# Two fused blocks on one core: priorities at the norm boundaries, and new places for masks, norm rows, zero stores and decay scalars

## The chip, the cores and the metric

The kernel runs on one core of a Trainium2 chip. The metric is device time in microseconds of one execution. The kernel before has a median of 932.28 us over three runs, between 931.84 and 934.05.

## The reference

One sequence of 256 tokens, each of 1024 float32 values, goes through two blocks. The first has attention with a relative bias and a gated delta rule beside it, both from one projection, then an MLP with squared relu. The second has a short convolution and a retention mixer, then a gated MLP. In short:

```python
# first block
h    = rms_norm(x, pre_mix_norm)
proj = h @ w_in                       # att q,k,v; gdn q,k,v; z; a; b
o    = concat(attention(att_q, att_k, att_v, rel_bias), gated_deltanet(...))
x    = x + rms_norm(o @ w_out, post_mix_norm)
x    = x + rms_norm(square(relu(rms_norm(x, pre_mlp_norm) @ w_up)) @ w_down, post_mlp_norm)
# inside gated_deltanet, in chunks of 64 tokens, 8 heads of 64
q, k, v = split(silu(causal_conv(qkv)))
q, k    = l2_normalize(q) / 8, l2_normalize(k)
g       = -exp(A_log) * softplus(a + dt_bias);  beta = sigmoid(b)
m       = strict_lower((k * beta) @ k.T * decay(g))
u, w    = solve(I + m, [v * beta, k * beta * exp(cumsum(g))])
# then a scan over the chunks: state, v_new = u - w @ state, output
# second block
h = rmsnorm(x, g_mix);  proj = h @ w_in_2
y_a = (gb * conv3(gc * xc)) @ w_a_out
y_r = (groupnorm(retention(rotary(q), rotary(k), v, log_sigmoid(dec_f), log_sigmoid(dec_b))) * g_ret * silu(g_sw)) @ w_r_out
x = x + (sigmoid(gate_a) * y_a + sigmoid(gate_r) * y_r) @ w_o
h = rmsnorm(x, g_ffn);  x = x + (silu(h @ w_ff_gate) * (h @ w_ff_up)) @ w_ff_down
return rmsnorm(x, g_final)
```

## The kernel before

Every matrix product is made of three: a float32 operand is split into a rounded part and a remainder, hi and lo, and hi*hi, hi*lo and lo*hi are added in PSUM (mm3, L222 and L294). Weights come in chunks of 512 KB. load_w (L208) issues the transfer to the tile raw on SyncE's queue, ScalarE copies raw to wh (the rounded part), VectorE subtracts to get wl (the remainder). Three buffers hold raw, six each wh and wl, so the transfer of a chunk starts when ScalarE and VectorE are through with the third chunk before it.

A scheduler puts the instructions of the whole program in order on each engine by priority, which falls with the place in the source; an engine then works through its own list strictly in order. Two things bend this order. `with after("x")` orders an instruction behind the one last recorded as `last["x"]` without making it wait for data (L170). And side work, the products of attention and of later projections, is cut into steps that go("q") or go(number) places between the steps of the mixer (the FILL list). The gates GATE_H and GATE_L order the splits of the first five chunks, the fifth behind the decay scalars g of the delta rule.

The mixer of the first block, 0 to about 190 us, runs as follows. The activations are normalised and transposed to xT. Projections for k and q are convolved (acc), turned back to tokens, squared (sq), summed (ssq, ssk), and their reciprocal norms are a power on POOL (rstd, L400: ms on VectorE, then rnk or rnq on POOL). VectorE forms m from the k products; m goes through DRAM (md) and comes back as mb, in blocks of 16. POOL scales k (kbe, kd, L876) and multiplies m with two level masks per token tile (b, L895, four instructions). VectorE scales q (fq, fqd, qn, qd) and solves the 16 by 16 blocks by substitution in 30 small steps (tmpb and tb, L937). The solution goes through the DRAM scratches td and ud and comes back as T and U (L947), for the products that join the blocks. Of td and ud only the diagonal blocks are written there; the zeros are stored at L828 from a tile of zeros, 520 KB each. A store to and a load from the same scratch are ordered by semaphores.

At three boundaries a product is followed by a norm whose result the next product needs: w_out to w_up (L1071), w_down to w_in_2 (L1120) and w_o_2 to the gated MLP (L1282). For each of the two token tiles, post_norm_add (L454) squares the sums on ScalarE, takes a power on POOL and adds to x on VectorE; rms_T (L444) repeats this for x and transposes the result on TensorE; split_T makes hi and lo on ScalarE and VectorE (xT, L413 and L416). The norm weights are rows broadcast over 128 partitions, two transfers of 256 KB each (row_bcast, L178), on POOL's queue, ordered behind the last power ("pow").

The logarithm of the second block's decays (log1p_exp_neg_abs, L497) stands behind the w_up products in the source; its ScalarE steps need a table for Ln, which a table load brings in.

Of the kernel before, what the change touches and what calls it, by code (L numbers as in the profile page):

```python
# [13 lines left out]
AF = mybir.ActivationFunctionType  # L14
ALU = mybir.AluOpType
# [82 lines left out]
def body(ctx: ExitStack, tc: tile.TileContext, I: dict, cst: bass.AP, out: bass.AP, dbg=None):  # L98
# [47 lines left out]
    def tt(o, a, b, op, eng=None):  # L146
        (eng or nc.vector).tensor_tensor(o, a, b, op=op)  # L147
# [21 lines left out]
    @contextmanager  # L169
    def after(what):  # L170

        if what in last:
            with tc.issue_after(last[what].ins):
                yield
        else:
            yield

    def row_bcast(name, eng=None):  # L178
        a = I[name]
        h = [xpool.tile([P, 512], F32, tag="wb", name=nm("wb"), bufs=4) for _ in range(2)]  # L180
        with after("pow"):
            for i in range(2):
                (eng or nc.gpsimd).dma_start(h[i], bass.AP(tensor=a.tensor, offset=a.offset + i * 512,
                                                           ap=[[0, P], [1, 512]]))
        return h
# [21 lines left out]

    def load_w(w, k0, nk, c0, ncol):  # L208
        raw = wpool.tile([P, nk, ncol], F32, tag="raw", name=nm("raw"), bufs=RBUFS)
        nc.sync.dma_start(raw, w[k0 * P:(k0 + nk) * P, c0:c0 + ncol].rearrange("(k p) n -> p k n", p=P))  # L210
        H = wpool.tile([P, nk, ncol], F32R, tag="wh", name=nm("wh"), bufs=WBUFS)
        L = wpool.tile([P, nk, ncol], F32R, tag="wl", name=nm("wl"), bufs=WBUFS)
        n = len(started)
        started.append(1)
        with after(GATE_H[n] if n < len(GATE_H) else None):
            act(H, raw, AF.Copy)
        with after(GATE_L[n] if n < len(GATE_L) else "sub"):
            last["wl"] = nc.vector.tensor_tensor(L, raw, H.bitcast(F32), op=SUB)  # L218
        return H, L
# [180 lines left out]
    def rstd(o, ss, n, dim):  # L400
        ms = sm("ms", n)
        nc.vector.tensor_scalar(ms, ss, 1.0 / dim, EPS, op0=MUL, op1=ADD)
        tt(o, ms, neghalf[:, :n], ALU.pow, nc.gpsimd)

    def split_T(ps, X, k0, t, scale=None):

# [35 lines left out]
        return xs  # L442

    def rms_T(xt, wb, X, t):  # L444
        row_T(rms_row(xt, wb, t in FUSED), X, t)

    def row_T(row, X, t):
        for i, xs in enumerate(row):
# [3 lines left out]
            split_T(ps, X, 4 * i, t)  # L452

    def post_norm_add(ps, wb, xt):  # L454
        r = rms_of(ps)
        tmp = [T2("pw", tag="n") for _ in range(2)]
        for i in range(2):
            tt(tmp[i], ps[i], wb[i], MUL)
        for i in range(2):
            stt(xt[:, GS[i]], tmp[i], r, xt[:, GS[i]], MUL, ADD)  # L460

    xr = [rms_row(x[:, t, :], wb_pre, True, None) for t in range(2)]
    C0 = T2("cs")
# [28 lines left out]
        return h  # L492

    hs = head_scalars(("A_log", "dt_bias"))
    load_consts(0, NMIX)

    def log1p_exp_neg_abs(src, n):  # L497

        a, u, w, l, d, rw = (sm("lp" + c, n) for c in "auwldr")
        act(a, src, AF.Abs)  # L500
        act(u, a, AF.Exp, scale=-1.0)
        nc.vector.tensor_scalar(w, u, 1.0, None, op0=ADD)
        last["ln"] = nc.scalar.activation(l, w, AF.Ln)
        stt(d, w, -1.0, u, ADD, SUB)
        nc.vector.reciprocal(rw, w)
        tt(d, d, rw, MUL)
        tt(l, l, d, SUB)
        return l
# [315 lines left out]


    KBE, KD, KT_, MM, BL = [], [], [], [], []
    for d in (td, ud):
        nc.sync.dma_start(d[:, :].rearrange("p (r n) -> p r n", r=5),  # L828
                          zero[:, None, :208].to_broadcast([P, 5, 208]))
    pk = [tok_major(2, t) for t in range(2)]  # L830
    rk = [inv_norm(pk[t], "k") for t in range(2)]
    go(FILL[2])
# [40 lines left out]
    for t in range(2):  # L873
        kbe, kd = G2("kbe"), G2("kd")
        tt(h8(kbe), h8(kn[t]), hb(tile_h(FB, t)), MUL, nc.gpsimd)
        tt(h8(kd), h8(kn[t]), hb(tile_h(ER, t)), MUL, nc.gpsimd)  # L876
        KBE.append(kbe)
        KD.append(kd)

    go("q")  # L880
    go(FILL[4])
    VB, AT, QDT = [], [], []
    pq = [tok_major(0, t) for t in range(2)]
    rq = [inv_norm(pq[t], "q") for t in range(2)]
# [6 lines left out]
    for t in range(2):  # L891
        bl = []
        for s in (16, 32):
            b = G2("b")
            tt(h8(b), h8(MM[t]), cb(f"lev{s}"), MUL, nc.gpsimd)  # L895
            bl.append(b)
        BL.append(bl)

# [167 lines left out]
    wout.rows(mix, 0, range(WT0, 8), True)  # L1066
    wout.rows(mix, 1, range(wout.k, 8))
    ps = wout.ps
    wb1, wb2 = row_bcast("post_mix_norm"), row_bcast("pre_mlp_norm")
    X = Both("xT")  # L1070
    for t in range(2):  # L1071
        post_norm_add(ps[t], wb1, x[:, t, :])
# [18 lines left out]
    for i in range(4, 16):  # L1091
        hf = G2("hf")

        def up_evac(i=i, hf=hf):
            r = G2("relu")
            act(r, hf, AF.Relu)
            stt(hf, hf, 0.0, r, MAX, MUL)
            hv = hf.rearrange("p (j n) -> p j n", j=2)
            act(hid.h[i], hv, AF.Copy)
            tt(hid.l[i], hv, hid.h[i].bitcast(F32), SUB)  # L1100

        gemm_wide(I["w_up"][0], 256 * i, X, hf, up_evac)
    load_consts(NMIX, 3)

    dl = head_scalars(("dec_f_2", "dec_b_2"))
    lg = sm("lg", 8)
    lp = log1p_exp_neg_abs(dl, 8)
    stt(lg, dl, 0.0, lp, ALU.min, SUB)
# [173 lines left out]
    for t in range(2):  # L1282
        for i in range(2):
            gs = slice(i * 512, (i + 1) * 512)
            tt(x[:, t, gs], ps[t][i], x[:, t, gs], ADD)
        rms_T(x[:, t, :], wb1, X, t)
    dump("x3", x[:, 0, :])

# [92 lines left out]
```

## Time and profile before

| what | value |
|---|---|
| median of three runs | 932.28 us |
| profiled execution | 932.19 us |
| its span | 930.4 us |
| mean granted TensorE clock | 0.994 |
| TensorE busy | 902.0 us, 97% |
| VectorE busy | 600.1 us, 64% |
| ScalarE busy | 475.2 us, 51% |
| POOL busy | 81.2 us, 9% |

The span is the time between the first and the last instruction that the profile shows; the profiled execution is 1.79 us longer. Busy shares are means over a span with stages of different limits. What an engine waits for is in the list of waits and, for single places, in the timeline, where the time in square brackets is the idle time before an instruction and the name behind the arrow what ended it. PE is TensorE, DVE is VectorE, ACT is ScalarE, SP is SyncE; a granted clock of 1.00 is 2.4 GHz and of 0.50 is 1.2 GHz.

### The profile page before, as it was taken

Reading aid. Unit: us, or ns where it says so; the run is one execution under the profiler, and the core shown is the slowest. Engines: PE = TensorE matmul, PEld = TensorE weight load, DVE = VectorE, ACT = ScalarE, POOL = GpSimd, SP = SyncE. Lnnn points to the kernel's source line nnn. Section 1 sums busy time; section 2 is a strip of 40 time slices with the busy share of each in tenths; the row PEclk is TensorE's granted clock in tenths of the full one; section 3 lists DMA queues with packets and bytes.
Section 4 is the critical chain, followed back from the end, with each engine's and each line's share of the span. In section 5 each row is a group of like instructions: output and inputs, shape, how many; then the busy total and the mean of one; then the engine's idle time right before and its main releaser. Section 6 shows DMA issues by size and latency. Waiting matters only on the chain.

```text
span 930.4 us, 13880 instructions
## 1 busy us (share of the span) xinstructions
PE 902.0 (97%) x5397; PEld 770.2 (83%) x5397; DVE 600.1 (64%) x885; ACT 475.2 (51%) x722; POOL 81.2 (9%) x96
## 2 busy tenths in 40 slices
PE   5999999989999999999999999999999999999997
PEld 4788887778888888799988888888888788888886
DVE  3888555376887563868666687844557657666543
ACT  4774373356766453645445555444344546555432
POOL 4072001030000000203200000000000000000000
PEclk9999999999999999999999999999999999999999
DMA  9673663147676665577646457666474567666551
GB/s 274 183 184 67 161 211 91 46 144 209 193 203 203 222 196 182 155 220 214 182 119 176 132 165 201 181 203 190 165 229 141 159 203 205 189 191 184 183 179 46
DMA packets 177138, 162.41 MB, mean 175 GB/s; under 512 B 18940, under 2 KB 144168, under 8 KB 177072
## 3 DMA queue, kind: packets, MB, share of 16 engines
q1 hardware_dynamic: 175200, 156.49, 57.3%
q0 software_dynamic: 1728, 4.78, 1.6%
q8 instruction: 42, 0.69, 0.3%
q10 hardware_dynamic: 144, 0.26, 0.1%
q14 instruction: 24, 0.20, 0.1%
HBM read 158.59 MB, written 2.92 MB: 174 GB/s over the span
## 4 chain that ended last, share of the span: by engine, by line
PE 85%; DMA 4%; POOL 3%; ACT 3%; DVE 3%; issue 2%; SPq 0%; POOLq 0%; ACTq 0%
PE mm L222 57%; PE at L222 18%; PE sd L222 6%; PE mm L294 2%; DMA raw<-in_w_in_dram 1%; POOL b L147 1%; ACT junk L424 1%; DVE wl L218 1%; PE sd L795 1%; POOL r L428 1%; DMA rows<-in_w_conv_dram 1%; DMA raw<-in_w_up_dram 1%; ACT wh L144 1%; DMA wb<-in_pre_mlp_norm_dram 1%; DMA x<-in_x_dram 0%
## 5 line engine op out<-in xcount | busy, mean ns | idle before, releaser
L218 DVE TENSOR_TENSOR wl<-raw,wh 128x1024 fp32r<-128x1024 f32 (+1 forms) x287 | 352.3, 1232 | 220.7 <-ACT wh L144 218.8
L144 ACT ACTIVATE wh<-raw 128x1024 fp32r<-128x1024 f32 (+1 forms) x287 | 301.8, 1056 | 293.5 <-PE at L222 69.5
L222 PE MATMUL mm<-xT,wh 128*128 128x256 f32 (+1 forms) x976 | 251.5, 334 | 1.4 <-ACT wh L144 1.4
L222 PEld LDWEIGHTS mm<-xT,wh 128*128 128x128 f32 x976 | 167.2, 193 | 21.0 <-ACT wh L144 1.6
L222 PE MATMUL mm<-wh,xT 128*128 128x512 f32 x528 | 168.6, 393 | 2.6 <-DVE xT L416 1.5
L222 PEld LDWEIGHTS mm<-wh,xT 128*128 128x128 f32 x528 | 98.7, 188 | 25.3 <-DVE xT L416 2.8
L222 PE MATMUL mm<-xT,wl 128*128 128x256 f32 x400 | 111.9, 280 | 0.0
L222 PE MATMUL mm<-wl,xT 128*128 128x512 f32 x264 | 103.5, 392 | 0.6 <-DVE wl L218 0.6
L222 PE MATMUL at<-xT,wh 128*128 128x512 f32 x272 | 97.4, 398 | 0.0
L294 PE MATMUL mm<-xT,wl 128*128 128x256 f32 x288 | 82.9, 288 | 1.2 <-DVE wl L218 1.2
L222 PE MATMUL at<-xT,wl 128*128 128x256 f32 x272 | 76.1, 280 | 0.0
L222 PEld LDWEIGHTS mm<-xT,wl 128*128 128x128 f32 x400 | 75.4, 189 | 0.0
L222 PE MATMUL mm<-wh,hidh 128*128 128x512 f32 x162 | 63.3, 391 | 0.0
L222 PE MATMUL mm<-wl,hidh 128*128 128x512 f32 x162 | 63.2, 390 | 0.0
L222 PE MATMUL mm<-wh,hidl 128*128 128x512 f32 x162 | 63.0, 389 | 0.0
L222 PEld LDWEIGHTS at<-xT,wh 128*128 128x128 f32 x272 | 51.1, 188 | 12.4
L222 PEld LDWEIGHTS mm<-wl,xT 128*128 128x128 f32 x264 | 49.6, 188 | 11.4 <-DVE wl L218 1.5
L294 PEld LDWEIGHTS mm<-xT,wl 128*128 128x128 f32 x288 | 56.5, 196 | 1.6 <-DVE wl L218 1.6
L222 PEld LDWEIGHTS at<-xT,wl 128*128 128x128 f32 x272 | 51.3, 189 | 0.0
L428 POOL TENSOR_TENSOR r<-ms,neghalf 128x1 f32<-128x1 f32 x13 | 10.7, 823 | 436.2 <-DVE ms L150 436.2
L222 PEld LDWEIGHTS mm<-wh,hidl 128*128 128x128 f32 x162 | 30.4, 188 | 6.5
L222 PEld LDWEIGHTS mm<-wh,hidh 128*128 128x128 f32 x162 | 30.5, 188 | 5.8
(378 smaller groups left out, 1237.9 us busy)
## 6 DMA issues: line engine op xcount, KB each, us to landing
raw<-in_w_in_dram SPq DMA_DIRECT2D x116, 512.0 KB, 4.5
raw<-in_w_up_dram SPq DMA_DIRECT2D x32, 512.0 KB, 4.4
raw<-in_w_down_dram SPq DMA_DIRECT2D x32, 512.0 KB, 3.8
raw<-in_w_ff_gate_dram SPq DMA_DIRECT2D x22, 512.0 KB, 4.1
raw<-in_w_ff_up_dram SPq DMA_DIRECT2D x22, 512.0 KB, 3.9
raw<-in_w_ff_down_dram SPq DMA_DIRECT2D x22, 512.0 KB, 3.5
raw<-in_w_r_out_dram SPq DMA_DIRECT2D x16, 512.0 KB, 4.2
raw<-in_w_out_dram SPq DMA_DIRECT2D x8, 512.0 KB, 3.8
```

The lines of the kernel that those rows point to most:

```text
L144: nc.scalar.activation(o, i, f, **kw)
L147: (eng or nc.vector).tensor_tensor(o, a, b, op=op)
L218: last["wl"] = nc.vector.tensor_tensor(L, raw, H.bitcast(F32), op=SUB)
L222: nc.tensor.matmul(o, a, b, start=start, stop=stop)
L294: last["step"] = nc.tensor.matmul(o, L[:, k, :], XH, start=False, stop=k == 7)
L424: last["sq"] = nc.scalar.activation(T2("junk", tag="j"), srcs[i], AF.Square, scale=1.0 / 32, accum_out=ss[:, i:i + 1])
L428: last["pow"] = nc.gpsimd.tensor_tensor(r, ms, neghalf[:, :1], op=ALU.pow)
L795: nc.tensor.transpose(ps[:, a * P:(a + 1) * P], src[:, a * P:(a + 1) * P], ident)
```

## The change

The change has five parts. (1) The four transfers of the norm rows of the first boundary are ordered behind the last kd on POOL, no longer behind an early power. (2) The zero stores of td and ud move from the k side to the q side of the mixer, behind the weight transfer that was issued last there. (3) The four mask products b are ordered behind the second power of q's norm. (4) The norm, the transposes and the splits at the boundaries, the residual sums after w_o_2 among them, are given high priority. (5) The decay scalars of the second block are loaded at the start, ahead of the constants, and the first step of a logarithm is ordered behind the last relu that was recorded before it.

```diff
@@ row_bcast
-    def row_bcast(name, eng=None):
+    def row_bcast(name, eng=None, gate="pow"):
...
-        with after("pow"):
+        with after(gate):
...
@@ load_w
-        nc.sync.dma_start(raw, w[k0 * P:(k0 + nk) * P, c0:c0 + ncol].rearrange("(k p) n -> p k n", p=P))
+        last["ld"] = nc.sync.dma_start(raw, w[k0 * P:(k0 + nk) * P, c0:c0 + ncol].rearrange("(k p) n -> p k n", p=P))
...
@@ rstd
-    tt(o, ms, neghalf[:, :n], ALU.pow, nc.gpsimd)
+    last["rstd"] = nc.gpsimd.tensor_tensor(o, ms, neghalf[:, :n], op=ALU.pow)
...
@@ rms_T
-        row_T(rms_row(xt, wb, t in FUSED), X, t)
+        with tc.high_priority():
+            row_T(rms_row(xt, wb, t in FUSED), X, t)
...
@@ post_norm_add: its body, unchanged, now stands inside
+        with tc.high_priority():
...
@@ before the constants are loaded
+    dl = head_scalars(("dec_f_2", "dec_b_2"))
     load_consts(0, NMIX)
...
-    dl = head_scalars(("dec_f_2", "dec_b_2"))
     lg = sm("lg", 8)
     lp = log1p_exp_neg_abs(dl, 8)
...
@@ log1p_exp_neg_abs
-        act(a, src, AF.Abs)
+        with after("relu"):
+            act(a, src, AF.Abs)
...
@@ the mixer, k side
-    for d in (td, ud):
-        nc.sync.dma_start(d[:, :].rearrange("p (r n) -> p r n", r=5),
-                          zero[:, None, :208].to_broadcast([P, 5, 208]))
     pk = [tok_major(2, t) for t in range(2)]
...
-        tt(h8(kd), h8(kn[t]), hb(tile_h(ER, t)), MUL, nc.gpsimd)
+        last["kd"] = nc.gpsimd.tensor_tensor(h8(kd), h8(kn[t]), hb(tile_h(ER, t)), op=MUL)
...
@@ the mixer, q side
     go("q")
     go(FILL[4])
+    with after("ld"):
+        for d in (td, ud):
+            nc.sync.dma_start(d[:, :].rearrange("p (r n) -> p r n", r=5),
+                              zero[:, None, :208].to_broadcast([P, 5, 208]))
...
             b = G2("b")
-            tt(h8(b), h8(MM[t]), cb(f"lev{s}"), MUL, nc.gpsimd)
+            with after("rstd"):
+                tt(h8(b), h8(MM[t]), cb(f"lev{s}"), MUL, nc.gpsimd)
...
@@ before the first norm boundary
-    wb1, wb2 = row_bcast("post_mix_norm"), row_bcast("pre_mlp_norm")
+    wb1, wb2 = (row_bcast(n, gate="kd") for n in ("post_mix_norm", "pre_mlp_norm"))
...
@@ up_evac
-            act(r, hf, AF.Relu)
+            last["relu"] = nc.scalar.activation(r, hf, AF.Relu)
...
@@ after w_o_2
-            tt(x[:, t, gs], ps[t][i], x[:, t, gs], ADD)
+            with tc.high_priority():
+                tt(x[:, t, gs], ps[t][i], x[:, t, gs], ADD)
```

On SyncE's queue, this is the start of the program before. raw is a weight chunk, td and ud are the scratches.

```order
L210 DMA raw_208<-in_w_in_dram 128x8x128
L210 DMA raw_273<-in_w_in_dram 128x8x128
L828 DMA td<-zero 640x1x208
L828 DMA ud<-zero 640x1x208
L210 DMA raw_315<-in_w_in_dram 128x8x128
L210 DMA raw_345<-in_w_in_dram 128x8x128
L210 DMA raw_407<-in_w_in_dram 128x8x128
L210 DMA raw_468<-in_w_in_dram 128x8x128
```

And this is the same queue now, from the fourth chunk on.

```order
L210 DMA raw_318<-in_w_in_dram 128x8x128
L210 DMA raw_348<-in_w_in_dram 128x8x128
L210 DMA raw_410<-in_w_in_dram 128x8x128
L210 DMA raw_469<-in_w_in_dram 128x8x128
L210 DMA raw_519<-in_w_in_dram 128x8x128
L210 DMA raw_587<-in_w_in_dram 128x8x128
L210 DMA raw_629<-in_w_in_dram 128x8x128
L210 DMA raw_659<-in_w_in_dram 128x8x128
L210 DMA raw_755<-in_w_in_dram 128x8x128
L885 DMA td<-zero 640x1x208
L885 DMA ud<-zero 640x1x208
L210 DMA raw_827<-in_w_in_dram 128x8x128
```

The two zero stores no longer stand behind the third chunk but behind the twelfth, and ahead of the thirteenth.

On POOL, this is the middle of the mixer before: kbe and kd scale k, b are the masks, rnq the norm of q.

```order
L147 TENSOR_TENSOR kbe_749<-kn_549,fb_581 128x512
L147 TENSOR_TENSOR kd_750<-kn_549,er_579 128x512
L147 TENSOR_TENSOR b_816<-m_699,cs_171 128x512
L147 TENSOR_TENSOR b_818<-m_699,cs_171 128x512
L147 TENSOR_TENSOR b_820<-m_722,cs_171 128x512
L147 TENSOR_TENSOR b_822<-m_722,cs_171 128x512
L147 TENSOR_TENSOR rnq_798<-ms_799,neghalf 128x8
L147 TENSOR_TENSOR rnq_806<-ms_807,neghalf 128x8
```

And now, with wb the norm rows:

```order
L147 TENSOR_TENSOR kbe_750<-kn_550,fb_582 128x512
L877 TENSOR_TENSOR kd_751<-kn_550,er_580 128x512
L183 DMA wb_2154<-in_post_mix_norm_dram 128x512
L183 DMA wb_2155<-in_post_mix_norm_dram 128x512
L183 DMA wb_2158<-in_pre_mlp_norm_dram 128x512
L183 DMA wb_2159<-in_pre_mlp_norm_dram 128x512
L403 TENSOR_TENSOR rnq_801<-ms_802,neghalf 128x8
L403 TENSOR_TENSOR rnq_809<-ms_810,neghalf 128x8
L147 TENSOR_TENSOR b_819<-m_700,cs_174 128x512
L147 TENSOR_TENSOR b_821<-m_700,cs_174 128x512
L147 TENSOR_TENSOR b_823<-m_723,cs_174 128x512
L147 TENSOR_TENSOR b_825<-m_723,cs_174 128x512
```

The norm rows come in behind kd, the two powers behind them, and the four mask products last.

On VectorE, at the m products of the mixer (wl is the remainder of a weight chunk, acc a convolution), the order before:

```order
L218 TENSOR_TENSOR wl_915<-raw_912,wh_914 128x1024
L218 TENSOR_TENSOR wl_987<-raw_984,wh_986 128x1024
L147 TENSOR_TENSOR m_699<-sd_700,eb_568 128x4x64
L147 TENSOR_TENSOR m_699<-sd_701,eb_568 128x4x64
L150 SCALAR_TENSOR_TENSOR acc_688<-mm_627,chan,acc_688 128x255 x2
L150 SCALAR_TENSOR_TENSOR acc_688<-mm_627,chan,acc_688 128x254 x2
L150 SCALAR_TENSOR_TENSOR acc_688<-mm_627,chan,acc_688 128x253 x2
L147 TENSOR_TENSOR m_722<-sd_723,eb_574 128x4x64
L147 TENSOR_TENSOR m_722<-sd_724,eb_574 128x4x64
L218 TENSOR_TENSOR wl_1020<-raw_1017,wh_1019 128x1024
```

And now:

```order
L218 TENSOR_TENSOR wl_830<-raw_827,wh_829 128x1024
L218 TENSOR_TENSOR wl_918<-raw_915,wh_917 128x1024
L147 TENSOR_TENSOR m_700<-sd_701,eb_569 128x4x64
L147 TENSOR_TENSOR m_700<-sd_702,eb_569 128x4x64
L147 TENSOR_TENSOR m_723<-sd_724,eb_575 128x4x64
L150 SCALAR_TENSOR_TENSOR acc_689<-mm_628,chan,acc_689 128x255 x2
L150 SCALAR_TENSOR_TENSOR acc_689<-mm_628,chan,acc_689 128x254 x2
L150 SCALAR_TENSOR_TENSOR acc_689<-mm_628,chan,acc_689 128x253 x2
L147 TENSOR_TENSOR m_723<-sd_725,eb_575 128x4x64
L218 TENSOR_TENSOR wl_990<-raw_987,wh_989 128x1024
```

One wl has moved from ahead of the m products to behind them, and the first m of the second token tile stands ahead of the convolution.

At the boundaries, TensorE's transposes of the first token tile (sd and at from ident and xs) stood behind the last matmul of the product before the boundary. They now stand ahead of its last 4 matmuls at w_out, 6 at w_down and 19 at w_o_2, all of them of the second token tile.

## Rows read from the trace of the kernel before

**Rows 1.** The page's busy times: us (share of the span) and instructions of each engine.

```profile
...
PE 902.0 (97%) x5397; PEld 770.2 (83%) x5397; DVE 600.1 (64%) x885; ACT 475.2 (51%) x722; POOL 81.2 (9%) x96
...
```

**Rows 2.** TensorE's waits over the span; us in total, times, longest us.

```profile
...
PE sd L451 <- DVE xs L439: 10.6, 3, 9.4
PE mm L222 <- DVE xT L416: 1.5, 3, 0.9
PE mm L222 <- ACT wh L144: 1.4, 1, 1.4
...
PE sd L795 <- DVE qn L147: 1.2, 1, 1.2
PE mm L294 <- DVE wl L218: 1.2, 2, 0.8
PE mm L222 <- ACT xT L413: 1.1, 3, 0.5
...
PE sd L222 <- DMA U<-ud: 0.6, 1, 0.6
...
```

**Rows 3.** Windows: width, busy PE PEld DVE ACT POOL (instructions), PEclk, DMA share, GB/s.

```profile
...
9.00:28.00 19.00, 16.03 (x109) 14.59 (x110) 11.12 (x28) 8.41 (x19) 7.65 (x15) 0.94 1.03 304
40.00:60.00 20.00, 19.49 (x193) 18.26 (x191) 15.43 (x27) 17.82 (x28) 10.24 (x8) 1.00 0.63 174
...
26.00:28.00 2.00, 2.00 (x11) 2.00 (x11) 1.12 (x7) 1.97 (x4) 0.00 (x0) 0.50 0.93 253
28.00:30.00 2.00, 1.75 (x10) 1.55 (x9) 1.93 (x4) 2.00 (x4) 0.00 (x0) 0.68 0.11 32
62.00:64.00 2.00, 2.00 (x23) 1.93 (x19) 2.00 (x6) 0.13 (x1) 2.00 (x4) 0.85 0.81 220
64.00:66.00 2.00, 2.00 (x11) 2.00 (x11) 2.00 (x4) 1.81 (x3) 2.00 (x3) 0.50 0.81 197
66.00:68.00 2.00, 2.00 (x16) 2.00 (x15) 2.00 (x2) 1.67 (x3) 2.00 (x2) 0.79 0.79 158
...
```

**Rows 4.** Timeline of TensorE and ScalarE; start us, us, engine, line, [idle before <-releaser].

```profile
...
23.87 0.50 PE L222 MATMUL mm<-xT,wh 128*128 128x256 f32 x2 [1.41 <-ACT wh L144]
...
61.50 0.96 PE L222 MATMUL sd<-kt 64*64 64x64 f32 x16 [1.32 <-DVE m L147]
...
22.76 1.06 ACT L144 ACTIVATE wh<-raw 128x1024 fp32r<-128x1024 f32 x1 [7.35 <-DMA raw<-in_w_in_dram]
...
```

**Rows 5.** DMA issues of 0 to 100 us; KB each, median us to landing.

```profile
...
td<-zero SPq DMA_DIRECT2D x1, 520.0 KB, 6.3
...
wb<-in_post_mix_norm_dram POOLq DMA_DIRECT2D x2, 256.0 KB, 6.4
...
```

**Rows 6.** Page group of wl; timelines of POOL and VectorE; the chain's two DMAs.

```profile
...
L218 DVE TENSOR_TENSOR wl<-raw,wh 128x1024 fp32r<-128x1024 f32 (+1 forms) x287 | 352.3, 1232 | 220.7 <-ACT wh L144 218.8
...
64.98 8.00 POOL L147 TENSOR_TENSOR b<-m,cs 128x512 f32<-128x512 f32 x4
72.94 3.24 POOL L147 TENSOR_TENSOR rnq<-ms,neghalf 128x8 f32<-128x8 f32 x2
...
64.70 3.63 DVE L218 TENSOR_TENSOR wl<-raw,wh 128x1024 fp32r<-128x1024 f32 x2
...
69.44 0.15 DVE L402 TENSOR_SCALAR ms<-ssq 128x8 f32<-128x8 f32 x1
...
71.75 1.25 DVE L402 TENSOR_SCALAR ms<-ssq 128x8 f32<-128x8 f32 x1
...
76.21 0.17 DVE L903 TENSOR_SCALAR fq<-rnq 128x8 f32<-128x8 f32 x1 [0.79 <-POOL rnq L147]
...
78.84 0.17 DVE L147 TENSOR_TENSOR tmpb<-mb,tb 128x15 f32<-128x15 f32 x1
...
89.57 3.86 DMA ud<-ub
93.44 4.19 DMA U<-ud
...
```

More of the change, by code (lines that the diff above doesn't have):

```diff
@@ L454, in post_norm_add @@
     def post_norm_add(ps, wb, xt):
[L455 to L460, printed above, removed]
+        with tc.high_priority():
+            r = rms_of(ps)
+            tmp = [T2("pw", tag="n") for _ in range(2)]
+            for i in range(2):
+                tt(tmp[i], ps[i], wb[i], MUL)
+            for i in range(2):
+                stt(xt[:, GS[i]], tmp[i], r, xt[:, GS[i]], MUL, ADD)
     xr = [rms_row(x[:, t, :], wb_pre, True, None) for t in range(2)]
```

## The prediction

> **What bounds the kernel now.** I began with the engines' busy time. TensorE is busy 902.0 us of a span of 930.4 [rows 1], so an edit pays only where it removes a TensorE wait or a stretch at a low clock. The profiled execution took 932.19 us, 1.79 more than its span and 0.09 under the median of the three runs, 932.28; the sum is made against it and read as the median.
>
> The second view is TensorE's waits [rows 2]. The first line is 10.6 us in three times, the longest 9.4 us, at the start, where the first activations have to arrive; the change leaves those alone. What the change can reach is the rest: 1.4 for wh, 1.2 for wl, 1.2 for qn, 0.6 for U, 1.3 for m [rows 4], and around the three stage boundaries 1.5 and 1.1 for xT and the other 1.2 of the first line (10.6 − 9.4). That is 9.5 us.
>
> The third view, two-microsecond windows, shows what the waits list can't [rows 3]. Twice the granted clock falls to 0.50, which is 1.2 GHz, while TensorE is busy through the window: once in 26 to 28 us, once in 64 to 66. With the windows beside them the lost share is 0.50 + 0.32 and 0.15 + 0.50 + 0.21 of 2 us, so about 1.7 us each. Each fall comes behind a pause, of 1.41 us to 23.87 and of 1.32 us to 61.50 [rows 4]. The same windows show the DMA engines at 1.03 of their time through 9 to 28 us, at 304 GB/s, and at about 0.8 of it through 62 to 68.
>
> **The scratch zeros and the norm rows: the early stretch.** The wh at 22.76 sat behind a weight chunk for 7.35 us and TensorE then for 1.41 [rows 4]. In the saturated window the old kernel also moves td and ud (520 KB each) and four norm rows of 256 KB [rows 5], 2.06 MB. At 304 GB/s that is 6.8 us of DMA time, half of it (td and ud) issued directly ahead of the late chunk. Taking out td and ud alone brings this chunk 3.4 us forward, which is more than the 1.41 that TensorE waited. I therefore count the wh wait at 1.4 and both wl waits, which belong to the two chunks next in line, at 1.2 as gone, and the clock stretch that follows them, 1.7, with them: 4.3. What is late next is the chunk after it, whose split is ordered behind the decay scalars g; these follow the late chunk's wl on VectorE and come forward with it. The bounds are 0, if the weights stay behind something else in that queue, and 4.3.
>
> The Trainium skill (DMA: Bandwidth & Descriptors, Issuing engines are not separate DMA queues) says that transfers run on the same 16 engines and interleave, whoever issued them. By that rule the POOL-issued rows take time from the weights as td and ud do, and will do so again in their new place; the 1.03 of rows 3 agrees.
>
> td and ud now stand behind the loads for q, near 40 to 48 us. There the DMA engines are 0.63 busy over 20 us [rows 3], 7.4 us free against 3.4 needed: I count nothing, and up to 3.4 if a chunk queued behind them on SP is wanted at once. The norm rows now land at 62 to 70, where some 0.2 of 6 us, 1.2 us, is free and 3.4 is needed. They push weights or mb back by up to 2.2 us. POOL's own issue of four rows comes while rnq still waits for ms, and costs nothing.
>
> **The masks behind q's norm: the middle.** Here the chain was POOL's: b four times for 8.00 us, then rnq for 3.24, then fq, for which VectorE sat idle 0.79 [rows 6]; qn waited behind it. With rnq first, the qn wait of 1.2 goes. A wl also moves behind the m products in VectorE's order, so the m wait of 1.3 goes, and with the pause the second clock stretch, 1.7. TensorE by itself would gain 4.3 + 1.3 + 1.7 + 1.2 = 8.5 by here.
>
> But VectorE's own queue sets the solve. It is busy through all of 62 to 68 [rows 3], and its next idle time is that 0.79. What it gains is the 4.3 that its inputs come earlier, the 0.79, and what b cost it: two wl took 3.63 beside b where one takes 1.23 on average, 1.2 too long; and one ms took 1.25 where another took 0.15, 1.1 too long. A third wl in that stretch I put at half of the first two, 0.6. That is about 2.9 us over the 8.00. b now runs beside acc, qn and qd, which read PSUM. I count 2.9 less the 2.2 of the norm rows, so tmpb begins 4.3 + 0.8 + 0.7 = 5.8 earlier than 78.84. Behind it nothing shortens: ten microseconds of solve, the store of ud (3.86) and the load of U (4.19) [rows 6]. So U comes 5.8 us earlier, TensorE arrives 8.5 earlier, and its wait for U grows from 0.6 to about 3.3. The net is 5.8; bounds 1.5 (no early gain, the rest as counted) and 9.1 (U early enough too).
>
> The Trainium skill (SBUF — State Buffer, SBUF: two separate sides) speaks against this edit: a GpSimd instruction and a VectorE one with two SBUF operands exclude each other on one shared port for a whole instruction. The wl and ms rows beside b agree in direction. By the page b would cost tmpb and tb what it cost wl if it still runs then.
>
> **High priority at the boundaries.** The first tile's normalisation and transposes now stand 4, 6 and 19 matmuls ahead of where they stood. Those matmuls fill the waits for xT, 1.5 + 1.1 in six places. Nothing is removed from the second tile's chain, which is now late next: its squares and xs wait for the last matmuls, which are pushed back by the transposes. The 1.2 for xs at two boundaries may grow by what the first tile gains. I count 1.6 saved of the 3.8, nearer to the xT sum, since its cover is matmuls already loaded; bounds −0.5 and 3.0.
>
> **The early scalars and the table load.** Two small POOL transfers stand ahead of the constants and delay these by about 1.1 us; the constants are read later than that allows for, so nothing. The Ln table load leaves the first boundary for a place between the wide products, where ScalarE has slack: inside the 1.6.
>
> **Sum.** 5.8 + 1.6 = 7.4; I take 7.2, since the half-clock stretches are the least certain part, and 932.2 − 7.2 = 925.0.
>
> **The rivals.**
> *The early weights stay late* (0.22). For it: the queue is full from the first microsecond, and chunks behind the first one are near their need. Against: 3.4 us comes out directly ahead of the late one. Then only the wh wait's 1.4 of the 4.3 comes: the gain at U falls by 2.9 to 2.9, with 1.6 at the boundaries it is 4.5, and the time is 927.7; with none of the 4.3 and the boundaries at −0.5 it is 931.2.
> *TensorE's side holds everywhere* (0.16). U is not late: 8.5 and U's 0.6 come whole, with 1.6 that is 10.7, and the time 921.5. For it: the 2.2 of the norm rows may fall on weights that nobody awaits. Against: the solve and two transfers are unshortened.
> *The boundary edit only moves the wait* (0.10): 5.8 remains, 926.4. For it: the second tile's chain has the same length.
> *Slower: b beside the solve* (0.12). VectorE's tmpb and tb read SBUF twice, like wl. If they stand still while b runs, tmpb loses up to the 8.00 us of b. U would come 5.8 − 8.0, so 2.2 us later than before, after a pause of 8.5 + 2.2 on TensorE, and I add a new half-clock stretch of 1.7 behind it: 2.2 + 1.7 − 1.6 = 2.3 slower, 934.5. It decides from 5.8 us of loss on; rows 6 show 2.9 of 8.00 where wl was the partner, so it needs more than twice that. For it: wl's and ms's rows. Against: much of b falls beside PSUM readers.
>
> **How the numbers follow.** The forecast has 0.40, with its own range 922.5 to 928. The range 920 to 930.5 reaches over the first three rivals and leaves out the slower one and the tail of the first. A difference under 0.3%, 2.8 us, is what the runs can't tell from none. Faster by more: 0.40 + 0.16 + 0.10 and half of the first rival, 0.77. Within: the other 0.11 of the first rival and 0.05 of the slower one, 0.16. Slower by more: 0.07.
>
> **What would show it.** In the new profile wh near 22 us should not wait, the DMA share of 9 to 28 should fall below 0.9, and the granted clock of 24 to 30 and 62 to 68 should stay near 1. The waits for m and qn should be gone, and that for U should be the longest in the middle, about 3 us. rnq should follow ms at once, and wl beside b should read 1.2. At the boundaries the xT lines should shrink and xs stay. The forecast is wrong if the early wh still waits, if U does not grow while the time falls by less than 5, or if a weight or mb is late at 62 to 75 us.

## The result, and the profile after

The changed kernel takes 929.07 us, the median of six runs (925.96 to 930.63), against 933.41 for the kernel before, the median of six beside them. The ratio is 0.995 with an interval of 0.9931 to 0.9969, so a gain of 4.3 us, 2.9 to 6.4 by the interval. Timed a second time the same kernel took 926.47 (ratio 0.9916, 0.989 to 0.9943), a gain of 7.5. Both are faster by more than 0.3%, and both lie in the range of 920 to 930.5; the forecast was 925.0. The profiled execution of the changed kernel took 929.08 us with a mean granted clock of 0.993. The profiled execution of the kernel before took 932.19, so what the two traces have to explain is 3.1 us.

TensorE's waits in the changed kernel, the view of [rows 2]: us in total, times, longest us.

```profile
PE sd L452 <- DVE xs L439: 10.0, 4, 8.9
PE sd L222 <- DMA U<-ud: 2.1, 1, 2.1
PE mm L222 <- DVE wl L218: 1.6, 4, 0.8
PE sd L452 <- DVE xs L441: 1.2, 3, 0.5
PE sd L799 <- DVE qn L147: 1.0, 1, 1.0
PE sd L799 <- ACT qt L144: 0.9, 1, 0.9
PE at L222 <- ACT aqk L144: 0.9, 1, 0.9
PE sd L222 <- DVE m L147: 0.8, 1, 0.8
```

The wh line of 1.4 and both xT lines, 1.5 and 1.1, are gone. U has grown from 0.6 to 2.1 and is the longest wait after the start. The waits for m and qn have shrunk instead of going, and qt, a new name, has joined them. At the boundaries TensorE now waits for wl, 1.6 in four places, and for the xs of the first token tile (L441), 1.2 in three, where it waited for xT.

Windows of the changed kernel, columns as in [rows 3].

```profile
9.00:28.00 19.00, 18.86 (x138) 17.43 (x139) 15.55 (x37) 11.94 (x23) 7.28 (x13) 1.00 0.86 215
26.00:28.00 2.00, 2.00 (x19) 2.00 (x18) 2.00 (x6) 1.06 (x1) 0.00 (x0) 1.00 0.76 209
64.00:66.00 2.00, 2.00 (x19) 2.00 (x18) 1.13 (x2) 0.00 (x0) 2.00 (x2) 1.00 1.08 370
92.00:94.00 2.00, 0.53 (x3) 0.44 (x3) 0.00 (x0) 1.05 (x2) 0.00 (x0) 0.64 1.22 200
94.00:96.00 2.00, 2.00 (x5) 1.61 (x6) 1.97 (x3) 0.49 (x2) 0.00 (x0) 0.50 1.08 205
96.00:98.00 2.00, 2.00 (x26) 1.35 (x27) 1.11 (x3) 1.45 (x7) 0.00 (x0) 0.50 0.97 139
98.00:100.00 2.00, 2.00 (x17) 1.66 (x14) 1.19 (x5) 1.01 (x3) 0.00 (x0) 0.65 0.94 313
130.00:132.00 2.00, 2.00 (x33) 1.67 (x35) 2.00 (x4) 0.68 (x2) 0.00 (x0) 0.53 0.69 271
132.00:134.00 2.00, 2.00 (x39) 1.56 (x38) 0.28 (x1) 1.24 (x4) 0.00 (x0) 0.62 1.00 329
```

The early window is no longer saturated (0.86 and 215 GB/s, where [rows 3] had 1.03 and 304). Both old stretches at 0.50 are gone: 26 to 28 and 64 to 66 stand at 1.00. But a longer one stands behind the wait for U, from 92.6 to 99.4, and another from 130.1 to 133.5. In the kernel before these places stood at full clock, as its windows show:

```profile
92.00:100.00 8.00, 7.39 (x61) 6.40 (x61) 5.89 (x13) 3.64 (x10) 0.00 (x0) 1.00 1.04 215
130.00:150.00 20.00, 19.38 (x198) 15.61 (x197) 9.46 (x17) 10.59 (x22) 1.22 (x2) 1.00 0.38 122
```

To see where time is gained and given back, take one instruction of TensorE in both traces and subtract the starts. First five places of the kernel before, then the same five of the changed one (timeline of TensorE: start us, us, engine, line, [idle before <-releaser]).

```profile
90.07 1.57 PE L222 MATMUL at<-aqk,aqk 64*128 64x128 f32 x8 [0.37 <-ACT aqk L144]
97.76 0.30 PE L222 MATMUL sd<-U,b 64*64 64x64 f32 x2 [0.60 <-DMA U<-ud]
105.55 1.15 PE L222 MATMUL sd<-T,Q 64*64 64x64 f32 x32
205.12 0.63 PE L451 MATMUL sd<-ident,xs 128*128 128x128 f32 x4 [0.79 <-DVE xs L439]
741.17 0.63 PE L451 MATMUL sd<-ident,xs 128*128 128x128 f32 x4
```

```profile
83.05 1.57 PE L222 MATMUL at<-aqk,aqk 64*128 64x128 f32 x8
93.47 0.45 PE L222 MATMUL sd<-U,b 64*64 64x64 f32 x2 [2.12 <-DMA U<-ud]
103.74 1.15 PE L222 MATMUL sd<-T,Q 64*64 64x64 f32 x32
201.05 0.63 PE L452 MATMUL sd<-ident,xs 128*128 128x128 f32 x4 [0.33 <-DVE xs L439]
737.32 0.63 PE L452 MATMUL sd<-ident,xs 128*128 128x128 f32 x4 [0.52 <-DVE xs L439]
...
742.20 0.50 PE L222 MATMUL mm<-wl,xT 128*128 128x512 f32 x1 [0.76 <-DVE wl L218]
```

The differences are 7.0, 4.3, 1.8, 4.1 and 3.9 us. TensorE itself is 7.0 ahead, U holds it to 4.3, the half clock takes that to 1.8, the first boundary gives 2.3 back, and behind the last place the wl of 742.20 costs 0.76.

The stretch between, answering to [rows 6]: POOL, VectorE and ScalarE of the changed kernel, then the two transfers of its chain.

```profile
62.27 4.18 POOL L403 TENSOR_TENSOR rnq<-ms,neghalf 128x8 f32<-128x8 f32 x2 [0.57 <-DVE ms L402]
64.87 0.17 DVE L909 TENSOR_SCALAR fq<-rnq 128x8 f32<-128x8 f32 x1 [1.47 <-POOL rnq L403]
66.42 5.00 POOL L147 TENSOR_TENSOR b<-m,cs 128x512 f32<-128x512 f32 x4
70.11 1.35 DVE L909 TENSOR_SCALAR fq<-rnq 128x8 f32<-128x8 f32 x1
70.23 1.06 ACT L144 ACTIVATE wh<-raw 128x1024 fp32r<-128x1024 f32 x1 [6.30 <-DMA raw<-in_w_in_dram]
73.78 0.17 DVE L147 TENSOR_TENSOR tmpb<-mb,tb 128x15 f32<-128x15 f32 x1
...
84.40 4.04 DMA ud<-ub
88.50 4.84 DMA U<-ud
```

tmpb begins at 73.78 instead of 78.84, 5.1 earlier. The load of U takes 4.84 instead of 4.19. b's four products take 5.00 instead of 8.00, and a weight chunk (wh at 70.23) waits 6.30 for its transfer.

### The profile page after: what moved, and what is told of

Its sections match the earlier page's. It is cut to its first block, busy times and chain, and to the rows that moved or that the text cites. A ratio compares the mean times of both kernels' runs of the same rounds, so it can differ in the third digit from the quotient of the medians.

```text
span 927.3 us, 13881 instructions
## 1 busy us (share of the span) xinstructions
PE 902.1 (97%) x5397; PEld 769.2 (83%) x5397; DVE 597.5 (64%) x885; ACT 476.4 (51%) x722; POOL 78.9 (9%) x96
## 4 chain that ended last, share of the span: by engine, by line
PE 84%; DMA 5%; DVE 5%; ACT 3%; issue 2%; POOL 1%; SPq 0%; POOLq 0%; ACTq 0%; DVEq 0%
PE mm L222 56%; PE at L222 17%; PE sd L222 7%; DMA raw<-in_w_in_dram 2%; PE mm L294 2%; DVE wl L218 1%; ACT wh L144 1%; POOL r L428 1%; PE sd L799 1%; ACT junk L424 1%; DMA raw<-in_w_ff_up_dram 1%; DMA wb<-in_pre_mix_norm_dram 1%; PE sd L452 1%; DMA U<-ud 1%; DMA raw<-in_w_out_dram 0%
## 5 line engine op out<-in xcount | busy, mean ns | idle before, releaser
L222 PE MATMUL mm<-xT,wh 128*128 128x256 f32 (+1 forms) x976 | 248.0, 331 | 0.0
L222 PEld LDWEIGHTS mm<-xT,wh 128*128 128x128 f32 x976 | 164.9, 190 | 19.2 <-issue 0.8
```

The costliest lines, as they stand in the source:

```text
L222: nc.tensor.matmul(o, a, b, start=start, stop=stop)
```

## The experiments

All kernels compute the whole reference. One table collects what the comparison of starts gives for the profiled executions: us by which TensorE starts the same matmul earlier than in the kernel before. Of what the changed kernel has, 0.4 us was there at the first matmul, and 0.1 when run again. The last row but one is 932.19 less the profiled time, the last the median's ratio.

| place (start in the kernel before) | changed | again | no priority | scalars late | vector masks, rows later |
|---|---|---|---|---|---|
| ahead of U (92.6) | 6.9 | 6.4 | 6.6 | 7.0 | 8.4 |
| first U product (97.8) | 4.3 | 3.3 | 3.9 | 4.5 | 7.5 |
| first T,Q product (105.6) | 1.8 | 0.7 | 4.0 | 3.1 | 7.5 |
| ahead of the first boundary (192) | 1.6 | 0.5 | 4.7 | 3.9 | 7.3 |
| behind it (232 to 256) | 4.2 | 3.2 | 6.7 | 1.7 | 9.9 |
| behind the second (417) | 4.3 | 3.6 | 7.0 | 2.1 | 10.2 |
| behind the third (781) | 3.1 | 3.6 | 7.1 | 1.7 | 10.0 |
| profiled execution | 3.1 | 3.6 | 7.1 | 1.7 | 10.0 |
| ratio | 0.995 | 0.9916 | 0.9954 | 0.9978 | 0.9869 |

**The changed kernel with the norm rows behind the last b.**

```
-                tt(h8(b), h8(MM[t]), cb(f"lev{s}"), MUL, nc.gpsimd)
+                last["b"] = nc.gpsimd.tensor_tensor(h8(b), h8(MM[t]), cb(f"lev{s}"), op=MUL)
-    wb1, wb2 = (row_bcast(n, gate="kd") for n in ("post_mix_norm", "pre_mlp_norm"))
+    wb1, wb2 = (row_bcast(n, gate="b") for n in ("post_mix_norm", "pre_mlp_norm"))
```

> The changed kernel with one edit: the four norm rows stand behind the last mask product b on POOL instead of behind kd. Theory A (the norm rows' megabyte at 60 to 70 us delays a weight chunk, and with it a wl, q's second tile and the solve): the wh that waits 6.3 us near 70 waits 3 us or less, tmpb begins near 71 to 72 instead of 73.8, the wait for U falls from 2.1 us to about 1 or less, and the half-clock stretch behind it shrinks or goes; time 1.5 to 4 us below the changed kernel, about 925 to 927.5. Rival B (the solve is late by its own length and the rows are beside the point): tmpb moves by less than 0.7 us, the wait for U stays near 2, and the time stays within 1 us of the changed kernel.

Measured: 926.96 us, ratio 0.9927 (0.9899 to 0.9955). Timeline of ScalarE, POOL and VectorE:

```profile
66.98 1.06 ACT L144 ACTIVATE wh<-raw 128x1024 fp32r<-128x1024 f32 x1 [1.06 <-DMA raw<-in_w_in_dram]
68.37 5.03 POOL L901 TENSOR_TENSOR b<-m,cs 128x512 f32<-128x512 f32 x4
72.13 2.35 DVE L218 TENSOR_TENSOR wl<-raw,wh 128x1024 fp32r<-128x1024 f32 x1
```

The chunk's wait fell from 6.30 to 1.06 us, so the rows were what delayed it. The solve did not gain: tmpb began at 75.68, 1.9 later than in the changed kernel. TensorE was 2.0 us later already at 43 us, ahead of the place of the edit, where an early chunk came later in this execution; and the chunk that is no longer late puts its wl beside b, where it took 2.35 instead of 1.2. The time lies between the two timings of the changed kernel. That the rows set the start of the solve is not shown by this run.

The Trainium skill (SBUF — State Buffer, SBUF: two separate sides) says that a GpSimd instruction that reads SBUF and a VectorE one with two SBUF inputs lock each other out of a shared port for a whole instruction. The rows of operations with two such inputs agree: wl at 2.35 here, and the small fqd at 0.55 instead of 0.15 beside b in the changed kernel.

**The kernel before with the zeros' stores moved, and nothing else.**

```
-    for d in (td, ud):
-        nc.sync.dma_start(d[:, :].rearrange("p (r n) -> p r n", r=5),
-                          zero[:, None, :208].to_broadcast([P, 5, 208]))
...
+    with after("ld"):
+        for d in (td, ud):
+            nc.sync.dma_start(d[:, :].rearrange("p (r n) -> p r n", r=5),
+                              zero[:, None, :208].to_broadcast([P, 5, 208]))
```

> The kernel before with one part of the change: the zero stores of td and ud behind the loads on the q side (this also moves a wl behind the m products). Theory A (these stores alone make the early chunk late): TensorE is 3.5 to 4.6 us ahead at 43 us, with no half-clock stretch near 26, the m wait goes and the qn wait grows, because b still stands ahead of rnq; in the end 1 to 3 us faster than before. Rival (the norm rows hold the chunk back as much as the zeros): 1.5 to 2.5 us ahead at 43 us and the low clock stays.

Measured: 937.54 us, ratio 1.0041 (1.0023 to 1.006): slower. Timeline of ScalarE and TensorE:

```profile
17.65 1.06 ACT L144 ACTIVATE wh<-raw 128x1024 fp32r<-128x1024 f32 x1 [1.64 <-DMA raw<-in_w_in_dram]
26.31 1.06 ACT L144 ACTIVATE wh<-raw 128x1024 fp32r<-128x1024 f32 x1 [3.80 <-DMA raw<-in_w_in_dram]
27.42 0.51 PE L222 MATMUL mm<-xT,wh 128*128 128x256 f32 x2 [1.79 <-ACT wh L144]
```

The late chunk came early, at 17.65 instead of 22.76 [rows 4]. But a later chunk, at 26.31, waited 3.80, and TensorE waited 1.79 for it. TensorE was ahead by only 1.0 at 43 us. This is what I had claimed to be worth 4.3. The half clock near 26 was gone, as theory A has it, but the lead was below both expectations. In the end the kernel is slower, and its clock goes with that: in its trace, three stretches at half clock, from 61.1, 98.6 and 136.1 us on, have 20.5 us together, where the kernel before has 6.8. Ahead of the second TensorE had waited 2.4 for U.

**The kernel before with the norm rows moved behind kd, and nothing else.**

```
-        with after("pow"):
+        with after(gate):
...
-    wb1, wb2 = row_bcast("post_mix_norm"), row_bcast("pre_mlp_norm")
+    wb1, wb2 = (row_bcast(n, gate="kd") for n in ("post_mix_norm", "pre_mlp_norm"))
```

> The kernel before with one part of the change: the norm rows behind kd, nothing else; the scheduler then mixes them with b and rnq. Theory A (the zeros are the early cost): 0 to 1 us ahead at 43 us, the early wh wait and the low clock stay, and the end is within 1.5 us of before. Rival (the rows are half of the cost): 1.5 us or more ahead at 43 us and the low clock near 26 goes.

Measured: 933.97 us, ratio 1.0009 (0.9985 to 1.0033): no difference. At 43 us TensorE was 1.8 ahead, and the half clock near 26 was gone, which is what the rival says. In POOL's order, with b still ahead of the powers, the rows stood among b and rnq, and the wait for qn became 2.6. Zeros alone give 1.0 and rows alone 1.8 in the early stretch, in one trace each; with both, the changed kernel has 5.0 there and 4.3 when run again, and the other kernels with both 3.0 to 5.5. So the two are worth more together than the sum of each alone: one transfer's room is taken up by the other, and the wait goes to the next chunk until both are out. The Trainium skill (DMA: Bandwidth & Descriptors, Issuing engines are not separate DMA queues) has transfers of all issuers share the same 16 engines; POOL's rows taking up what SP's stores left agrees with it.

**The changed kernel without the high priority.**

```
-        with tc.high_priority():
+        if True:
```

at all three places.

> The changed kernel without any high priority; all else stays. Theory A (priority wins at the first boundary, nothing at the second, and loses about 1.2 us at the third, because it puts a wl behind the norm): up to 1.6 us slower than the changed kernel, with the loss at the first boundary and 1 us back at the third. Rival (the first boundary's 2.7 us came from the early decay scalars and the moved table load, not from priority): 0.5 to 1.5 us faster than the changed kernel, the first boundary unchanged.

Measured: 928.91 us, ratio 0.9954 (0.9931 to 0.9977): the same as the first timing with priority. The profiled execution is worth more than that. Up to the first boundary it is the same program, each engine in the same order, with the same wait for U, and it shows no half clock (timeline of TensorE, then windows):

```profile
93.89 0.30 PE L222 MATMUL sd<-U,b 64*64 64x64 f32 x2 [2.23 <-DMA U<-ud]
...
101.54 1.15 PE L222 MATMUL sd<-T,Q 64*64 64x64 f32 x32
```

```profile
94.00:96.00 2.00, 2.00 (x18) 1.40 (x19) 1.76 (x3) 0.70 (x2) 0.00 (x0) 1.00 0.91 190
96.00:98.00 2.00, 2.00 (x33) 1.75 (x30) 1.32 (x3) 1.24 (x6) 0.00 (x0) 1.00 1.07 181
```

From U to T,Q this execution takes 101.54 − 93.89 = 7.65 us, the changed one 103.74 − 93.47 = 10.27: the half clock there costs 2.6. By the first boundary the difference is 4.7 − 1.6 = 3.1, and 3.5 with the 0.4 by which it was behind at U. At the first boundary it gains 2.0, and nothing is lost at the third, as theory A has it. The execution took 925.11 at a granted clock of 0.999; the seven others of the same kernel took 927.64 to 933.71 at 0.990 to 0.995. They were not traced, so that they lost it at the same places is likely and not shown.

**The changed kernel with b on VectorE, behind the solve.**

```
-            with after("rstd"):
-                tt(h8(b), h8(MM[t]), cb(f"lev{s}"), MUL, nc.gpsimd)
+            with after("sub"):
+                tt(h8(b), h8(MM[t]), cb(f"lev{s}"), MUL)
```

> The changed kernel with the four mask products b on VectorE behind the last step of the solve, no longer on POOL beside q's scaling (the scheduler also puts one weight chunk behind the loads of U and T). Theory C (b on POOL takes VectorE's time: fq took 1.35 and fqd 0.55 us beside it, some 1.6 us ahead of tmpb): tmpb begins 1.0 to 1.7 us earlier against TensorE's transposes of y for q, and the wait for U falls from 2.1 us to about 1. Theory D (a late weight chunk and its wl set the start of the solve): tmpb begins within 0.5 us of where it did, and the wait for U stays at 2 or more. Either way VectorE has 2.7 us more behind the solve.

Measured: 924.49 us, ratio 0.9908 (0.988 to 0.9936). Timeline of VectorE:

```profile
72.00 1.23 DVE L218 TENSOR_TENSOR wl<-raw,wh 128x1024 fp32r<-128x1024 f32 x1 [2.15 <-ACT wh L144]
...
74.42 0.17 DVE L147 TENSOR_TENSOR tmpb<-mb,tb 128x15 f32<-128x15 f32 x1
```

tmpb came no earlier, at 74.42: the wl ahead of it waited 2.15 for the chunk that the norm rows delay (its wh, at 70.90, had waited 6.99). So with b away from POOL the late chunk holds the solve; in the changed kernel wl starts at 71.37, when both the wh of that chunk (71.29) and b (71.42) end. TensorE's wait for U was gone nevertheless, because TensorE itself was late: it had lost 2.0 to qt, then ran at half clock from 75 to 85, and came to the U products at 95.98, 2.5 later than in the changed kernel. The load of U was also shorter, 3.4 us in the median instead of 4.7; the last run but one below says what goes with it. Only this execution, of 926.30 us at 0.993, was traced; the three others, at 0.998, took 923.42 to 924.93.

**The changed kernel with the decay scalars and their logarithm back in their old place.**

```
-    dl = head_scalars(("dec_f_2", "dec_b_2"))
     load_consts(0, NMIX)
...
-        with after("relu"):
-            act(a, src, AF.Abs)
+        act(a, src, AF.Abs)
...
+    dl = head_scalars(("dec_f_2", "dec_b_2"))
     lg = sm("lg", 8)
```

> The changed kernel with part 5 undone: decay scalars loaded, and the logarithm taken, at the first boundary again. Theory (the first boundary's gain of 2.6 us is mostly the logarithm that left it, and priority gives the small rest): the gain between 192 and 232 us falls from 2.6 to 0.6 or less, and the end is about 2 us slower than the changed kernel at the same clock. Rival (priority makes it): the gain there stays at 2 or more, and the end within 0.7 us.

Measured: 931.05 us, ratio 0.9978 (0.9956 to 0.9999). Timeline of ScalarE and TensorE at the first boundary:

```profile
204.02 0.21 ACT L144 ACTIVATE lpa<-hs 128x8 f32<-128x8 f32 x1 [3.96 <-DMA hs<-in_dec_b_dram]
...
206.21 1.11 PE L797 MATMUL sd<-ident,hf 128*128 128x128 f32 x4 [3.19 <-DVE hf L150]
```

ScalarE stands 3.96 us at the head of its queue for the scalars' transfer, hf comes late, and TensorE waits 3.19. At this boundary the changed kernel gains 2.7 on the kernel before; this one loses 2.2, a stretch of 3.4 us at half clock from 206 on included. In the kernel before the same step of ScalarE stood 2.95 us, and TensorE did not wait behind it:

```profile
209.39 0.21 ACT L144 ACTIVATE lpa<-hs 128x8 f32<-128x8 f32 x1 [2.95 <-DMA hs<-in_dec_b_dram]
```

So the late scalars cost more here than they did before. Whether this is by the new order or by the transfers, which took 5.6 to 6.0 us to land instead of 3.8 to 4.5, is not shown: no run has the late scalars without the priority. With the changed kernel's priority, the scalars' early load, which I priced inside the 1.6, is what lets the boundary's edit pay.

**The changed kernel with b ahead of q's norm again.**

```
-            with after("rstd"):
-                tt(h8(b), h8(MM[t]), cb(f"lev{s}"), MUL, nc.gpsimd)
+            tt(h8(b), h8(MM[t]), cb(f"lev{s}"), MUL, nc.gpsimd)
```

> The changed kernel with part 3 undone: b four times ahead of rnq on POOL, the norm rows behind b. Theory (rnq behind b puts the solve off): fq waits for POOL, tmpb begins 3 to 5 us later than in the changed kernel, the wait for qn grows past 2 us or that for U past 3, and 2 to 4 us are lost by 105 us. Rival (VectorE's own queue sets the solve either way): tmpb within 1 us, less than 1 us lost.

Measured: 930.01 us, ratio 0.9969 (0.9946 to 0.9991). The wait for qn was 4.7, with 3.4 us of half clock behind it from 73.5 on, and tmpb began at 75.79, 2.0 later than in the changed kernel. Three of the four norm rows stood ahead of b on POOL and one between b and rnq. Ahead of U, TensorE was 3.3 ahead of the kernel before instead of 6.9. The move is worth 3.6 on TensorE's side, the half clock included, and 2.0 on the solve's.

**The changed kernel again.** Nothing is edited.

> The changed kernel, unaltered, once more. Theory (the low clock falls by chance behind a pause of some 2 us, and a kernel with the same waits has it in one execution and not in another): the waits of TensorE agree within 0.5 us with the first profile, but the half-clock stretches at 92.6 (6.8 us) and 130.2 (3.4 us) are shorter, elsewhere or missing, and the span moves with them by 1.5 to 5 us. Rival (they belong to this program): both stretches are there again, within 1 us of the same place.

Measured: 926.47 us, ratio 0.9916 (0.989 to 0.9943); the profiled execution took 928.56 at a clock of 0.993. It waited 2.7 for U and ran at half clock again from 93.8 to 100.6 and from 131.3 to 134.7: the same two stretches, as long as before and 1.2 us later. So this trace stands nearer to the rival than to the theory; that a kernel with the same wait can go without them rests on the trace without priority. The wl of the third boundary cost nothing this time. The other five executions, at 0.996 to 0.998, took 923.46 to 927.15. In the first timing four executions at 0.992 to 0.994 took 929.06 to 930.63, and two at 0.997 took 925.96 and 927.67. So the two timings differ as their clocks do.

**b on VectorE, the norm rows behind both powers, priority at the first boundary alone.** The run with b on VectorE left the rows' traffic ahead of the solve, so here the rows move too.

```
+    last["rq"] = last["rstd"]
...
-            with after("rstd"):
-                tt(h8(b), h8(MM[t]), cb(f"lev{s}"), MUL, nc.gpsimd)
+            with after("sub"):
+                tt(h8(b), h8(MM[t]), cb(f"lev{s}"), MUL)
...
-    wb1, wb2 = (row_bcast(n, gate="kd") for n in ("post_mix_norm", "pre_mlp_norm"))
+    wb1, wb2 = (row_bcast(n, gate="rq") for n in ("post_mix_norm", "pre_mlp_norm"))
...
+    PRIO[0] = False
     wb1, wb2 = row_bcast("post_mlp_norm"), row_bcast("g_mix_2")
```

> The kernel with the masks on VectorE behind the solve, with two more edits: the norm rows stand behind the two rnq on POOL instead of behind kd, and high priority is kept at the first boundary alone. Theory D (in the run before, a weight chunk held back by the norm rows set the start of the solve: wl waited 2.15 us): with the rows later that wait falls below 1 us, tmpb begins 1.5 to 2 us earlier than 74.4, the qt wait of 2.0 us falls below 1, and the time is 1 to 3 us below that kernel, 921.5 to 923.5. Rival (the rows only delay something else a little later): the wait moves, and the time stays within 1 us of 924.5.

Measured: 922.18 us (920.92 to 922.99), ratio 0.9869 (0.985 to 0.9888), the fastest kernel of the study. Timeline of VectorE and TensorE:

```profile
70.18 1.22 DVE L219 TENSOR_TENSOR wl<-raw,wh 128x1024 fp32r<-128x1024 f32 x1
...
72.59 0.18 DVE L147 TENSOR_TENSOR tmpb<-mb,tb 128x15 f32<-128x15 f32 x1
...
90.23 0.33 PE L223 MATMUL sd<-U,b 64*64 64x64 f32 x2 [0.41 <-DMA U<-ud]
...
98.07 1.08 PE L223 MATMUL sd<-T,Q 64*64 64x64 f32 x29
```

wl waits for nothing, tmpb is 6.3 earlier than before, the U products are 7.5 earlier and wait 0.41. No window before the end stands below full clock, and all five runs had 0.998 or 0.999. Of the lead of 7.5, 7.3 is kept to the boundary. Theory D's signs all came: the wait of wl, tmpb 1.8 earlier than in the run with b on VectorE, the wait for qt, and the time.

The solve is not all of it, though. Against the changed kernel tmpb is 1.2 earlier and the first U product 3.2, because the load of U is shorter (from the chain that ended last):

```profile
87.35 2.83 DMA U<-ud
```

It took 4.84 in the changed kernel. There SyncE issues a weight chunk at 86.40, between the store of ud and the load of U; here, as in the run with b on VectorE, the scheduler has put that chunk behind the loads of U and T. That this is why the load is shorter is likely: its four transfers took 3.4 us in the median in both kernels with that order, and 4.7 in the changed one. No run moves this chunk alone, so what the masks and the rows are worth without it is open.

**The same without any priority.** The three `with tc.high_priority()` are taken out; the rest is the edit above.

> As the kernel beside it, with no high priority at all. Theory (priority is worth about 0.6 us at the first boundary and nothing elsewhere): 0 to 1 us slower than the kernel beside it; between 192 and 232 us it gains about 2.0 where the other gains 2.6. Rival (priority matters by more than 1.5 us at the first boundary): 1.5 us or more slower.

Measured: 923.62 us (922.17 to 925.7), ratio 0.9886 (0.9865 to 0.9906). At the first boundary it gained 2.0 where the kernel above gained 2.6. The medians differ by 1.4 us, between the bounds of the theory and the rival, and the intervals overlap; from the two traces priority at the first boundary is worth 0.6.

## Why the prediction came out as it did

The direction and the range were right, and the likeliest case was the mechanism that happened: TensorE ahead of U, and the wait for U grown. The size was 7.2; the two timings gave 4.3 and 7.5, the two traces of the changed kernel 3.1 and 3.6. That the second timing comes near 7.2 is in part luck, as the terms show.

*The early stretch* had 4.3 and measured 5.0 and 4.3 at 43 us. The number is right by luck, and its working is wrong. I gave all of it to td and ud and made the rows no condition of it. Zeros alone give 1.0 and then a slower kernel, rows alone 1.8. The step "taking out td and ud alone brings this chunk 3.4 us forward, which is more than the 1.41 that TensorE waited" holds for that chunk, and not for the one behind it. Taking the next chunk in line as following was the mistake; the rows were in the queue until then.

*The waits for m and qn* had 1.3 and 1.2 as gone. They are 0.8 and 1.0, and qt has 0.9: ScalarE splits two chunks, from 70.23 and 71.71 on, ahead of it. The chunk at 70.23 waits for the rows, which I had charged to the solve alone. TensorE is 7.0 ahead at aqk instead of 8.5. The move of b ahead of the norm does what it was said to do: undone, qn waits 4.7.

*The U chain* had 5.8 and measured 4.3. tmpb is 5.1 earlier, 0.7 short, and the load of U takes 0.65 longer than in the kernel before. The wait for U is 2.1 and 2.7, predicted at about 3.3. The mechanism is right and its size is 1.5 too large; I had the two transfers unchanged.

*The clock* is the step that failed. The sum counts both stretches, 1.7 each, as gone with their pauses. They went from 26 and 64 us. Yet the forecast lets TensorE wait about 3.3 for U, which is a longer pause than the 1.41 and 1.32 behind which the half clock stood before [rows 3, 4], and puts no price on it; I had priced a new stretch only in the slower rival. It came: 6.8 us of half clock from 92.6 and 3.4 from 130.1. That takes the lead from 4.3 at U to 1.6 at the first boundary. The run without priority shows what stands in its place where the clock holds: 4.7 at the boundary and 925.11 at the end. That this is within 0.1 of the forecast is luck too: it has 3.9 at U instead of 5.8, 0.8 between U and the boundary where the sum has nothing, and 2.4 behind it instead of 1.6. The stretches that were removed early were in good part paid again behind the wait that the change made.

*The boundaries* had 1.6 in all. The changed kernel gained 2.7, 0.1 and −1.2, which is 1.5, and 2.6, 0.4 and 0.1 when run again, which is 3.1. So 1.6 was met by luck: the gain is at one boundary, and most of it is the scalars' move and not the priority: without the scalars' move it is a loss of 2.2, without the priority a gain of 2.0. At the third boundary the waits for xT, 0.62, became waits for xs of 1.00 us, and priority pushed a wl back, for 0.76 of TensorE's time in one trace and nothing in the other.

*The rivals.* That the early weights stay late did not happen with both edits in, and did with the first alone. That TensorE's side holds everywhere needed U to be early; it took two more edits, and a chunk that moved behind the load of U with them, and then gave 922.2, near the 921.5 of that rival. That b stands beside the solve and makes the kernel slower was wrong: b runs from 66.42 to 71.42 and tmpb from 73.78. Its four products even took 5.00 instead of 8.00; most of their partners on VectorE read PSUM here, which is the likely reason and not tested. What it cost was 1.2 of an fq and 0.4 of an fqd.

*Of the signs named ahead*, the DMA share below 0.9 (0.86), the clock at 24 to 30 and 62 to 68, rnq directly behind ms (POOL was idle until ms came), U as the longest wait in the middle and the xT lines gone were seen. m and qn were not gone, and at the boundaries xs did not stay, it grew from 1.2 to 2.3. One sign of being wrong was seen: a weight was late at 62 to 75 us, the wh at 70.23, by 6.30. wl beside b was not seen in the changed kernel, where wl starts at 71.37 as b ends; where it did stand beside b it took 2.35.

## What to carry to other kernels

When an edit takes work ahead of a wait off the path, put a price on the wait that grows in its place, the low clock behind it included; a pause that is moved can take its half-clock stretch along. In a full transfer queue the first late transfer is not the last: ask which is next, and which other transfer will take the room. An edit that brings the engine earlier to a boundary can make a transfer that stands there more costly, as that of the scalars here, so look whether it can move too.

## What the runs showed that was not expected

The half clock behind a pause does not come each time. The same program up to the first boundary waited 2.12, 2.65 and 2.23 us for U in three executions; two then ran at 0.50 for 6.8 us and one stayed at 1.00. Two kernels with the same order on TensorE, VectorE, ScalarE and SyncE up to there, the norm rows behind b and the scalars late, waited 2.44 and 2.06 and ran at 0.50 for 3.4 us each. From the first U product to T,Q the five took 10.27, 10.36, 7.65, 9.05 and 9.14 us, so a wait of this size cost between nothing and 2.7 us more. Executions of one kernel differ by as much: 925.11 at a mean clock of 0.999 and 933.71 at 0.990. What decides it is open: one trace was taken of each. The Trainium skill (TensorE: Matmul & The Clock Gate, Part 1: The HAM clock gate) says that the gate looks at activity in a rhythm that does not start with the kernel, and that the place where the clock first rises therefore varies from run to run. Executions that differ as these do would fit such a rhythm; but here it is a fall in the middle of the kernel, and they do not prove it.

VectorE's very small operations also stand still beside POOL: fq, on 128x8 elements, took 1.35 us beside b, and 0.17 at the same place in the run with b on VectorE. And POOL's four products on 128x512 took 8.00 us beside wl and ms, and 5.00 beside operations that read PSUM.
